# Turns of the identity on TensorE between the spread of g_mix and the first product

## The chip, the cores and the metric

The kernel runs on one core of a Trainium2 chip. The metric is the device time of one execution in microseconds (us). An execution taken with the hardware profiler gives a trace beside its time. "TensorE" multiplies matrices, "VectorE", "ScalarE" and "GpSimd" work on elements, and "SyncE" (SP) issues most of the DMAs; the profile calls them PE (PEld for its weight loads), DVE, ACT, POOL and SP.

## What is computed

One inference step of a trunk of one layer, for a prompt of 2048 frames and a running stream of 32 further frames, 1024 channels each. Cut to what matters here:

```python
hn = rmsnorm(h, g_mix)                 # y = x * rsqrt(mean(x*x) + EPS) * g_mix
proj = hn @ w_in                       # 1024 -> 3072, split into hA, bA, cA, zA, vB, zB
yA, new_conv = short_conv_mixer(hA, bA, cA, zA, conv_hist, conv_w, conv_b)
yB, new_pool = pooling_mixer(vB, zB, pool_hist, pos, pool_w, pool_scale)
h = h + concatenate([yA, yB]) @ w_out
gate = sigmoid(rmsnorm(h, g_ple) @ w_ple_gate)
h = h + (p @ w_ple) * gate             # then a last rmsnorm with g_final
```

The change touches only the beginning: the first `rmsnorm` and the way to the first matmul of `hn @ w_in`.

## The kernel before

**Precision and products.** All inputs are float32. An operand of a product is kept as two float32r numbers, a high half (a cast on ScalarE, line 78) and the rest (a subtraction on VectorE, line 79); the helper `split` makes both and `put` does it for a whole tile. A product then takes three matmuls for each chunk of 128 channels: high with high, high with rest, rest with high. In the input projection the weights stand in the array and 416 frames (`NB`) stream past them.

**Stages.** The 2080 frames are five blocks of 416, in groups of two, two and one (line 26). For each group the program goes through four units (128 channels of each mixer); the first unit of the first group is computed plainly, product by product (`Unit.plain`, line 783): zb and v for the first block, c, then zb, v, c for the second one, then h, za and b for both. Later units use a scheme of seven products for eight. Behind the input projection come the output projection and the gate. TensorE's work is one long row of products from the first one on.

**The beginning.** g_mix is read as one row and spread over the 128 partitions by a matmul with a row of ones, half by half, into `g_bc` (lines 369 to 377):

```python
373   for half in range(2):
374       cs = slice(half * NH, half * NH + NH)
375       pg = tbank(f"gm_{half}")
376       nc.tensor.matmul(pg, ones, gm_row[:, cs], start=True, stop=True)
377       nc.vector.tensor_copy(g_bc[:, cs], pg)
```

The first block is four columns of frames: three of 128 and a short one that holds 32 frames of the first block and 32 of the second (`short0`). Each column is loaded (`x_load`), its sum of squares is taken on ScalarE (line 89) and made into a root on GpSimd (lines 70 and 74), and VectorE scales it by the root and by `g_bc` (`normal`, line 407). TensorE then turns it, since a product needs channels on the partitions: four turns of 128x128 for each half of the channels go into one bank (`turn`, line 416), and `put` splits the bank into the high and low halves in `B0`:

```python
595   for c, x in enumerate([*ahead0, short0]):
596       normal(x)
597       n = P if c < 3 else DEC
598       for half, q in enumerate(("11", "21")):
599           put(B0[q][:, :, :, c * P:c * P + n], turn(x, half, f"pt0_{c}_{half}", bank)[:, :, :n])
```

The first product (`project`, line 581, zb) reads all four columns. It takes its 24 matmuls in the order high-high, frames' rest, weights' rest; all later ones (line 564) go chunk by chunk. The weights of the first three products are split at line 604, behind the columns.

**The second block.** `second_block` (line 610) takes the statistics of three more columns, scales them on VectorE (pinned in order), turns them between the first products of unit 0, splits each bank and also copies it out on ScalarE (line 627).

**PSUM.** There are eight banks: six called "mm" (`bank`, lines 50 and 54) for products and the turns of the two first blocks, and two called "tr" (`tbank`, lines 51 and 57) for the spread of g_mix, the vectors' turn and the pooling products. A bank is handed out again when all its readers are done.

**What sets the order.** Nothing is written out by engine: a scheduler orders the instructions of each engine from the program's order, the dependencies and its own estimate of durations, and places the waits. `tc.keep_in_program_order(ins)` pins an instruction: pinned instructions of an engine keep the order in which the program names them. The function `turn` has the parameter `later`, which pins its turns; the first block's turns don't use it, the second block's do.

Of the kernel before, what the change touches and what calls it, by code (L numbers as in the profile page):

```python
# [15 lines left out]
P = 128  # L16
# [19 lines left out]
def trunk(ctx, tc, x_p, x_s, c_conv, c_pool, p_p, p_s, g_mix, w_in, conv_w, conv_b, pool_w,  # L36
          pool_scale, w_out, g_ple, w_gate, w_ple, g_fin, y_p, y_s, sc_p, sp_p, sc_s, sp_s):
    nc = tc.nc
# [17 lines left out]
    def tbank(name):  # L56
        return ps_t.tile([P, 512], F32, tag="tr", name=name)

    ident = const.tile([P, P], F32, name="ident")
# [17 lines left out]
    def split(hi, lo, src, eng=nc.vector):  # L77
        ins = nc.scalar.copy(hi, src)  # L78
        eng.tensor_tensor(lo, src, hi.bitcast(F32), op=ALU.subtract)
        return ins  # L80
# [24 lines left out]
    def embed(todo, wp, ring, queue=nc.sync):  # L105

        got = {}  # L110

        def prep(c):
            if c in got or c >= len(todo):
                return
            i = todo[c]
            r, n = tiles[i]
            if c % 4 == 0:
                pt = ring("p", i)
                m = min(4, len(todo) - c)
                full = [j for j in todo[c:c + m] if j < NT - 1]  # L120
                if full:
                    nc.sync.dma_start(pt.rearrange("p (a d) -> p a d", a=4)[:, :len(full)],
                                      p_p[r:r + len(full) * P].rearrange("(a p) d -> p a d", p=P))
                if len(full) < m:
                    nc.sync.dma_start(pt[:DEC, len(full) * PLE:(len(full) + 1) * PLE], p_s)
                got["p"] = pt
            pt = got["p"][:, (c % 4) * PLE:(c % 4 + 1) * PLE]
            pps = ring("pps", i)
            ptp = tbank(f"ptp_{i}")
            for k in range(2):  # L130
                nc.tensor.transpose(ptp[:, k * P:k * P + n], pt[:n, k * P:(k + 1) * P], ident[:n, :n])
            v = ptp.rearrange("p (k t) -> p k t", k=4)[:, :2, :n]
            split(pps[:, 0, :, :n], pps[:, 1, :, :n], v)
            got[c] = pps

        def run(c, last=False):
            i = todo[c]
            r, n = tiles[i]
            prep(c)
            prep(c + 1)  # L140
            prep(c + 2)
            pps = got[c]
            o = ring("out", i)
            for nh in range(2):
                cs = slice(nh * NH, nh * NH + NH)
                ps = bank(f"e_{i}_{nh}")
                embed_product(ps, pps, wp, cs, n)
                (nc.vector.tensor_copy if last and nh else nc.scalar.copy)(o[:n, cs], ps[:n])
            (nc.gpsimd if last else queue).dma_start(e_d[r:r + n], o[:n])

        return prep, run
# [141 lines left out]
    def slot(name):  # L293
        return acts[0].tile([P, SLOT], F32R, tag="hn", name=name)
# [30 lines left out]
    def load_rows(pool, name, i, pr, sa=None):  # L325
        r, n = tiles[i]
        t = ring4(pool, f"{name}_{i}")
        nc.sync.dma_start(t[:n], pr[r:r + n] if sa is None else rows_of(pr, sa, r, n))
        return t

    with ExitStack() as s1:
# [10 lines left out]
        def piece_of(t, i):  # L342

            return t[:, i * PIECE:(i + 1) * PIECE].rearrange("p (k h n) -> p k h n", k=KH, h=2)
# [4 lines left out]
        def put(piece, src):  # L349

            return split(piece[:, :, 0], piece[:, :, 1], src)
# [30 lines left out]
        def x_rows(tb, c):  # L382
            r = tb * NB + c * P
            if c < 3:
                return x_p[r:r + P]
            return x_p[r:r + DEC] if tb < 4 else x_s
# [15 lines left out]
        def x_tile(name, rows, squares=junk):  # L402
            return x_stat(x_load(name, rows), squares=squares)

        def normal(x, later=False):
            xt, n, r = x
            ins = nc.vector.scalar_tensor_tensor(xt[:n], xt[:n], r[:n], g_bc[:n], op0=ALU.mult, op1=ALU.mult)
            if later:
                tc.keep_in_program_order(ins)

        def turn(x, half, name, get=tbank, later=False):
            xt, n, _ = x
            pt = get(name)
            for k in range(KH):
                kk = half * KH + k
                ins = nc.tensor.transpose(pt[:, k * P:k * P + n], xt[:n, kk * P:(kk + 1) * P], ident[:n, :n])
                if later:
                    tc.keep_in_program_order(ins)
            return pt.rearrange("p (k t) -> p k t", k=KH)[:, :, :n]
# [70 lines left out]
        def six(g):  # L490

            B = {}
            for i, names in enumerate(SLOTS):
                t = slot(f"B{g}_{i}")
                B.update((q, piece_of(t, c)) for c, q in enumerate(names))
            return B
# [88 lines left out]
        B0 = {}  # L585
# [6 lines left out]
        ahead0 = [x_tile(f"0_{c}", [x_rows(0, c)], in_raw(kind)) for c, kind in enumerate(raw_of)]  # L592
        short0 = x_tile("0_3", [x_rows(0, 3), x_rows(1, 3)])
        B0.update(six(0))
        for c, x in enumerate([*ahead0, short0]):
            normal(x)
            n = P if c < 3 else DEC
            for half, q in enumerate(("11", "21")):
                put(B0[q][:, :, :, c * P:c * P + n], turn(x, half, f"pt0_{c}_{half}", bank)[:, :, :n])
        hn[0] = B0["11"], B0["21"]  # L600
        ahead1 = []
        made = []
# [578 lines left out]
    with ExitStack() as s2:  # L1181
# [112 lines left out]
        for i in range(0, NT - 1, 2):  # L1294
            with tc.issue_after(loaded[-1].ins):
                x = [load_rows(xh, "x", i + b, x_p) for b in range(2)] if i else [first_x, second_x]
# [4 lines left out]
            if last:  # L1301
                n = tiles[NT - 1][1]
# [6 lines left out]
            if last:  # L1309
                x = load_rows(xh, "x", NT - 1, x_p, x_s)  # L1310
# [27 lines left out]
        _, run = embed(rest_e, wp, ring)  # L1338
# [273 lines left out]
        n = tiles[NT - 1][1]  # L1612
# [62 lines left out]
```

## Time and profile before

| what | us |
|---|---|
| three runs | 922.54, 920.85, 921.94 (median 921.94) |
| profiled execution | 920.29 |
| its span, from its first to its last instruction | 918.5 |
| spread of g_mix on TensorE | begins at 2.41 |
| first turn of a column | begins at 8.44 |
| first matmul of the first product | begins at 15.39 |

Times of rows are microseconds from the start of the span. A row of the timeline has its start and length, the engine, the line of the kernel, the operation, what it writes and reads, the shapes, how many such instructions are merged (x8), and in brackets the idle time ahead of it with what ended it. The length of merged rows reaches to the end of the last one, and matmuls overlap. A row of the waits has who waited for whom: the sum in us, the number of times and the longest.

### The profile page before, as it was taken

How to read it: one execution, taken by the hardware profiler on the slowest of the kernel's cores; microseconds unless marked ns; L12 is line 12 of the kernel's file. 1: busy time of each engine (PE TensorE's matmuls, PEld its weight loads, DVE VectorE, ACT ScalarE, POOL GpSimd, SP SyncE). 2: the span in 40 equal slices, each digit the busy share in tenths (PEclk: the TensorE clock that was granted, in tenths of full speed). 3: DMA queues.
4: the chain of work that ended last, by engine and by line, in shares of the span. 5: the costliest groups of instructions: out<-in, count | busy, mean ns of one | idle time of the engine just before them, and what ended most of it. 6: DMA issues, size and time to landing. Idle time of an engine off the chain costs nothing.

```text
span 918.5 us, 12937 instructions
## 1 busy us (share of the span) xinstructions
PE 904.2 (98%) x4485; PEld 819.3 (89%) x4485; DVE 722.4 (79%) x1231; ACT 478.3 (52%) x883; POOL 150.8 (16%) x271
## 2 busy tenths in 40 slices
PE   7999999999999999999999999999999999999996
PEld 5999999999999999999999988888877868888885
DVE  6996989999488989785777679765554799888965
ACT  6744565554345555443545456334334786565555
POOL 4111322212001111000000011111111002233333
PEclk9999999999999999999999999999999999999998
DMA  8245695779935546357655359755785886799893
GB/s 267 80 151 150 163 270 161 201 206 314 415 113 164 184 157 191 110 177 274 200 172 168 130 186 303 260 191 177 247 229 158 290 262 167 187 230 241 210 258 103
DMA packets 140734, 186.37 MB, mean 203 GB/s; under 512 B 12060, under 2 KB 111260, under 8 KB 139389
## 3 DMA queue, kind: packets, MB, share of 16 engines
q1 hardware_dynamic: 120237, 126.33, 45.0%
q0 software_dynamic: 17696, 53.71, 20.1%
q10 hardware_dynamic: 2736, 5.51, 1.8%
q8 instruction: 35, 0.57, 0.3%
q14 instruction: 30, 0.25, 0.1%
HBM read 128.93 MB, written 56.56 MB: 202 GB/s over the span
## 4 chain that ended last, share of the span: by engine, by line
PE 97%; DVE 1%; issue 1%; ACT 0%; DMA 0%; POOL 0%; SPq 0%; ACTq 0%; DVEq 0%; POOLq 0%
PE x_o L168 9%; PE x_g L168 9%; PE x_zbv L564 7%; PE x_ch L564 7%; PE x_zab L564 7%; PE e L103 5%; PE z_g L168 5%; PE z_o L168 4%; PE z_zbv L564 3%; PE z_ch L564 3%; PE z_zab L564 3%; PE v L564 3%; PE c L564 3%; PE b L564 3%; PE za L564 3%; PE h L564 3%
## 5 line engine op out<-in xcount | busy, mean ns | idle before, releaser
L78 ACT CAST y_S<-y_fS 128x512 fp32r<-128x512 f32 x32 | 19.3, 622 | 38.6 <-PE x_o L168 19.0
L103 PE MATMUL e<-wq,pps 128*128 128x512 f32 (+1 forms) x156 | 38.9, 400 | 0.2 <-ACT pps L78 0.2
L168 PE MATMUL x_o<-wo_b,y_S 128*128 128x512 f32 x128 | 35.8, 391 | 0.0
L168 PE MATMUL x_g<-wg_b,g_S 128*128 128x512 f32 x128 | 35.7, 389 | 0.0
L564 PE MATMUL z_zbv<-B,w_zbv_S 128*128 128x416 f32 x168 | 34.2, 352 | 0.0
L564 PE MATMUL x_ch<-B,w_ch_S 128*128 128x416 f32 x168 | 34.1, 351 | 0.0
L564 PE MATMUL z_zab<-B,w_zab_S 128*128 128x416 f32 x168 | 34.1, 351 | 0.0
L564 PE MATMUL x_zab<-B,w_zab_S 128*128 128x416 f32 x168 | 34.0, 351 | 0.0
L564 PE MATMUL x_zbv<-B,w_zbv_S 128*128 128x416 f32 x168 | 34.0, 351 | 0.0
L564 PE MATMUL z_ch<-B,w_ch_S 128*128 128x416 f32 x168 | 34.0, 351 | 0.0
L103 PEld LDWEIGHTS e<-wq,pps 128*128 128x128 f32 (+1 forms) x156 | 27.4, 182 | 7.0 <-ACT pps L78 0.5
L1402 POOL DMA_DIRECT2D e<-h_d x28 | 24.8, 906 | 52.9 <-DVE e L1399 45.9
L564 PEld LDWEIGHTS x_zab<-B,w_zab_S 128*128 128x128 f32 x168 | 31.3, 188 | 0.4
L564 PEld LDWEIGHTS x_zbv<-B,w_zbv_S 128*128 128x128 f32 x168 | 31.4, 188 | 0.3
L564 PEld LDWEIGHTS z_ch<-B,w_ch_S 128*128 128x128 f32 x168 | 31.4, 188 | 0.3
L564 PEld LDWEIGHTS z_zab<-B,w_zab_S 128*128 128x128 f32 x168 | 31.3, 188 | 0.3
L564 PEld LDWEIGHTS x_ch<-B,w_ch_S 128*128 128x128 f32 x168 | 31.3, 188 | 0.3
L564 PEld LDWEIGHTS z_zbv<-B,w_zbv_S 128*128 128x128 f32 x168 | 31.3, 188 | 0.4
L70 POOL TENSOR_SCALAR ms_x<-ssq_x 128x1 f32<-128x1 f32 (+2 forms) x18 | 11.0, 610 | 123.2 <-ACT junk L89 118.7
L78 ACT CAST y<-y 128x512 fp32r<-128x512 f32 x24 | 14.8, 618 | 29.2 <-PE x_o L168 14.6
L78 ACT CAST g_S<-g_fS 128x512 fp32r<-128x512 f32 x32 | 19.0, 618 | 18.5 <-DVE g_fS L1578 11.9
L168 PEld LDWEIGHTS x_o<-wo_b,y_S 128*128 128x128 f32 x128 | 24.0, 188 | 5.1 <-ACT c_o L1205 0.3
(598 smaller groups left out, 2651.5 us busy)
## 6 DMA issues: line engine op xcount, KB each, us to landing
y<-y_d SPq DMA_DIRECT2D x16, 512.0 KB, 5.6
x<-in_x_prompt_dram SPq DMA_DIRECT2D x16, 512.0 KB, 5.6
h_d<-x SPq DMA_DIRECT2D x16, 512.0 KB, 2.6
hn<-h_d SPq DMA_DIRECT2D x61, 128.0 KB, 6.2
xt<-in_x_prompt_dram SPq DMA_DIRECT2D x15, 512.0 KB, 5.4
e<-e_d SPq DMA_DIRECT2D x15, 512.0 KB, 6.4
e<-h_d POOLq DMA_DIRECT2D x28, 256.0 KB, 6.5
out_dram<-e POOLq DMA_DIRECT2D x13, 512.0 KB, 4.2
```

Source lines behind the costliest of these rows:

```text
L70: nc.gpsimd.tensor_scalar(ms[:n], ssq[:n], scalar1=1.0 / D, scalar2=EPS, op0=ALU.mult, op1=ALU.add)
L78: ins = nc.scalar.copy(hi, src)
L103: nc.tensor.matmul(ps[:n], pps[:, a, k, :n], wp[k][b][:, cs], start=k + q == 0, stop=k == 1 and q == 2)
L168: nc.tensor.matmul(ps[:n], lhs[:, k, a, :n], w[b][:, k], start=start and k + q == 0, stop=k == KH - 1 and q == 2, skip_group_check=True)
L564: nc.tensor.matmul(ps[:, :NB], lhs[:, k, x], b[:, k, y], start=start and k + q == 0, stop=stop and k == KH - 1 and q == 2, skip_group_chec ...
L1402: nc.gpsimd.dma_start(ee, h_d[r:r + P, at[1] * NH:at[1] * NH + NH], accum_op=ALU.add)
```

## The change

A bank `idle` is taken from the two "tr" banks, and a function `keep_busy(n)` turns the identity into it n times; nobody reads the result. Ten such turns are placed ahead of the first block's columns, and 5, 8, 10 and 2 behind the turns of the first, second, third and fourth column. They are pinned in the program's order, and so are the turns of the first block's columns from now on.

```diff
         B0.update(six(0))
+        idle = tbank("idle")
+
+        def keep_busy(n):
+
+            for _ in range(n):
+                tc.keep_in_program_order(nc.tensor.transpose(idle[:, :P], ident, ident))
+
+        keep_busy(10)
         for c, x in enumerate([*ahead0, short0]):
             normal(x)
             n = P if c < 3 else DEC
             for half, q in enumerate(("11", "21")):
-                put(B0[q][:, :, :, c * P:c * P + n], turn(x, half, f"pt0_{c}_{half}", bank)[:, :, :n])
+                put(B0[q][:, :, :, c * P:c * P + n], turn(x, half, f"pt0_{c}_{half}", bank, True)[:, :, :n])
+            keep_busy((5, 8, 10, 2)[c])
         hn[0] = B0["11"], B0["21"]
```

## The prediction

> **What bounds the kernel now.** I read the page first, then the waits of TensorE, then its timeline of the first 50 us.
>
> ```profile
> span 918.5 us, 12937 instructions
> PE 904.2 (98%) x4485; PEld 819.3 (89%) x4485; DVE 722.4 (79%) x1231; ACT 478.3 (52%) x883; POOL 150.8 (16%) x271
> ```
> ```profile
> PE gm L376 <- DMA gm_row<-in_g_mix_dram: 2.4, 1, 2.4
> PE pt L416 <- DVE xt L407: 2.3, 1, 2.3
> PE pt L416 <- issue: 1.3, 1, 1.3
> PE x_zab L564 <- DVE U L880: 0.3, 1, 0.3
> PE e L103 <- ACT pps L78: 0.2, 1, 0.2
> ```
> TensorE is busy for 904.2 of 918.5 us. All its waits but the last two, 0.5 us together, lie at the beginning. So whatever makes TensorE's stream earlier after the beginning comes out at the end nearly one for one, and whatever is won ahead of that and met again by another wait is lost.
>
> ```profile
> 2.41 3.75 PE L376 MATMUL gm<-gm_row,ones 1*128 1x512 f32 x4 [2.41 <-DMA gm_row<-in_g_mix_dram]
> 8.44 4.87 PE L416 MATMUL pt<-ident,xt 128*128 128x128 f32 x24 [2.29 <-DVE xt L407]
> 14.61 0.68 PE L416 MATMUL pt<-ident,xt 64*128 64x64 f32 x8 [1.29 <-issue]
> 15.39 2.88 PE L581 MATMUL zb<-B,w_firstzb 128*128 128x416 f32 x8
> 18.07 0.55 PE L564 MATMUL v<-B,w_firstv 128*128 128x416 f32 x1
> 18.41 3.51 PE L581 MATMUL zb<-B,w_firstzb 128*128 128x416 f32 x16
> 21.77 4.50 PE L564 MATMUL v<-B,w_firstv 128*128 128x416 f32 x23
> 26.20 2.60 PE L416 MATMUL pt<-ident,xt 64*128 64x64 f32 x24
> ...
> 28.67 2.52 PE L564 MATMUL c<-B,w_firstc 128*128 128x416 f32 x12
> ...
> 34.17 4.70 PE L564 MATMUL zb<-B,w_firstzb 128*128 128x416 f32 x24
> 38.71 4.70 PE L564 MATMUL v<-B,w_firstv 128*128 128x416 f32 x24
> ```
> The spread of g_mix ends at 2.41 + 3.75 = 6.16 us; the first product, zb, begins at 15.39. Between them stand the turns of four columns of frames, with idle time ahead of them. The second zb product takes 38.71 - 34.17 = 4.54 us for 24 matmuls, 0.189 each. The first one, at 15.39, takes 21.77 - 15.39 = 6.38 us for its 24 and one of v. The windows say why.
>
> ```profile
> 5.48:8.90 3.42, 1.13 (x3) 1.00 1.02 294
> 8.90:12.31 3.41, 3.38 (x17) 1.00 1.16 315
> 12.31:15.72 3.41, 2.01 (x18) 1.00 1.11 346
> 15.72:19.13 3.41, 3.41 (x12) 0.50 0.72 251
> 19.13:22.54 3.41, 3.41 (x20) 1.00 0.77 220
> ```
> The columns are the stretch, its length, TensorE's busy time with its matmuls, the granted clock, the DMA share and GB/s. For 3.41 us, just while the first product runs, the clock is 0.50. The stretch ahead of it, equally long, had TensorE busy for 2.01 of 3.41 us; the stretch ahead of the recovery, for all of it. The column reads 1.00 before that as well, but the weight loads of the turns contradict it:
>
> ```profile
> 10.17 1.57 PEld L416 LDWEIGHTS pt<-ident,xt 128*128 128x128 f32 x8 [0.16 <-DVE xt L407]
> 12.17 0.90 PEld L416 LDWEIGHTS pt<-ident,xt 128*128 128x128 f32 x8 [0.43 <-DVE xt L407]
> 14.57 0.57 PEld L416 LDWEIGHTS pt<-ident,xt 64*128 64x128 f32 x8 [1.50 <-issue]
> ```
> The second column of frames is turned at 1.57 / 8 = 0.20 us a turn, the third at 0.90 / 8 = 0.11, for the same shape. So I read the clock as half from the beginning to about 12.3, full to 15.72 because 8.90 to 12.31 was busy (3.38 of 3.41 us, with turns alone), half again because 12.31 to 15.72 was not, and full from 19.13. The change wants to fill the idle time so that the clock is up before 15.39 and stays up.
>
> The Trainium skill (TensorE: Matmul & The Clock Gate, Part 1) says that the clock is set by a free-running window of about 3.4 us of activity. The stretch of 3.41 us at 0.50 agrees.
>
> **The change part by part.**
>
> *The fill.* Ten turns of the identity follow the spread: at the half-clock price they end at 6.16 + 10 x 0.20 = 8.16, before the first column is ready at 8.44. The stretch 5.48 to 8.90 then holds about 3.1 us of work, and I take the clock to be full from 8.90. The first column: three turns at 0.20 and five at 0.11, to 9.6; five more of the identity to 10.15; the second column from 10.17 to 11.07; eight to 11.95; the third from 12.17 to 13.07; ten to 14.17; the fourth from 14.57 to 15.14; two to 15.36. Each batch ends before the row that follows it in the trace, so the fill costs nothing as long as it runs at 0.11. If the clock rises only at 12.31, each turn of the fill costs 0.20 until then: the second column starts at 10.04 + 1.0 = 11.04 and the first product about 0.9 us late, near 16.3, but warm. What is queued behind a turn of the identity on TensorE is the next column's turns; for those wait ScalarE's casts, VectorE's rests and in the end the product.
>
> Pinning the eight turns of each column into the program's order changes nothing in the sequence that the trace shows. The bank `idle` takes the seat of the first half of the spread; VectorE's copy out of that one must be done, which it is at 5.18:
>
> ```profile
> 4.49 0.69 DVE L377 COPY g_bc<-gm 128x512 f32<-128x512 f32 x1 [2.30 <-PE gm L376]
> ```
> No DMA, no ScalarE and no VectorE instruction is added.
>
> *The first product.* With a full clock, its first eight matmuls run from 15.39 to 15.39 + 8 x 0.189 = 16.90. The next eight read the low halves of the frames, and the last eight the low halves of the weights:
>
> ```profile
> 14.43 2.86 DVE L79 TENSOR_TENSOR B<-pt,B 128x512 fp32r<-128x512 f32 x6
> 17.22 1.27 DVE L79 TENSOR_TENSOR w_firstzb<-raw_firstzb,w_firstzb 128x512 fp32r<-128x512 f32 x2
> ```
> The last low half of the frames is there at 17.29, the one that the first four need a little earlier; I take 17.1. So the second eight end at 18.6, where the weights' rest is already there (18.49), and the third eight at 20.1. The early matmul of v fits into the wait at 16.9. Then v goes on at 20.15 in place of 21.77: 1.6 us are won here. VectorE thus takes back some of what the clock alone would give.
>
> *What is late next.* v's 23 matmuls take 26.20 - 21.77 = 4.43 us, to 24.6; the turns of the second block and the vectors' turn 28.67 - 26.20 = 2.47 us, so c could begin at 27.05. It can't. There are six product banks (line 50): zb, v and six banks of turns have been handed out, so c takes the first bank of turns, and that one must have been read by VectorE and ScalarE. VectorE, however, hangs on another chain:
>
> ```profile
> 25.04 0.55 POOL L74 TENSOR_TENSOR rstd_x<-ms_x,nhalf 128x1 f32<-128x1 f32 x1
> ```
> ```profile
> 25.62 1.28 DVE L407 SCALAR_TENSOR_TENSOR xt<-xt,rstd_x,g_bc 128x1024 f32<-128x1024 f32 x1 [0.72 <-POOL rstd_x L74]
> 26.84 0.59 DVE L752 TENSOR_TENSOR win<-V 128x416 f32<-128x416 f32 x1
> 27.35 0.28 DVE L79 TENSOR_TENSOR B<-pt,B 128x128 fp32r<-128x128 f32 x1
> ...
> 32.95 0.69 DVE L79 TENSOR_TENSOR B<-pt,B 128x512 fp32r<-128x512 f32 x1
> ```
> ```profile
> 28.10 0.28 ACT L627 COPY xt<-pt 128x128 f32<-128x128 f32 x1
> ```
> The last scaling of the second block waits for GpSimd's root at 25.59, which no matmul feeds. It ends at 26.90 whatever TensorE does, and VectorE's work is queued behind it. It reads the bank until 27.63; ScalarE's copy out of the same bank, at 28.10 now, can follow at 27.65 and end at 27.95. So c begins at 28.0 in place of 28.67, and 0.7 of the 1.6 us are left. The second zb product would start at 33.5 in place of 34.17, and its second matmul reads the low half that VectorE finishes at 32.95 + 0.69 = 33.64 now, up to 0.15 earlier when ScalarE's casts come earlier. That leaves 0.5 to 0.7 us; I take 0.6. From there on VectorE's rows have room, and TensorE's only further waits are the 0.5 us above, for results that come from its own products: they move with it.
>
> *Sum.* The profiled execution took 920.29 us, of which the span is 918.5; less 0.6 it is 919.7. The median of the three runs is 921.94, 1.65 above the profiled execution; I take the gain over as it is: 921.3 us. What a measurement of this kernel can tell from no change is about 0.2%, 1.8 us: this gain is below it.
>
> **The unknown price.** No row shows a turn of the identity by itself. The nearest rows are the turns of frames, 0.11 and 0.20 us; I take these. Whether it raises the clock like a turn of frames has two ends. The rows of 8.90 to 12.31 say yes: turns alone, and the loads fall from 0.20 to 0.11. The spread of g_mix, busy from 2.41 to 6.16, says that busy time isn't all: the turns at 8.44 and 10.17 still were slow. It has one row of the array at work, though (1x512), where a turn of the identity has all 128, mostly with zeros. I stay with the nearer row, the turns.
>
> **Rivals.**
>
> *All 1.6 us pass through.* If VectorE's order is drawn up otherwise once TensorE's stream is another (the low halves of the second block ahead of the pooling of v, say), the bank and the second product are freed earlier. Against it stands GpSimd's root at 25.59. Time: 921.94 - 1.6 = 920.3.
>
> *Nothing is won.* The change of clock has its own rhythm of 3.41 us, which need not stand to the program as it does in the profiled execution. Where a stretch ends near 14, it holds most of the second and all of the third column's turns, the clock rises there, and the next stretch, with 15.39 to 17.4 at work, may keep it up: then the old kernel had no cold product. Such runs gain nothing, and if the median run is one, or the bank of c is freed no earlier, the time is 921.9.
>
> *Slower: the fill doesn't count as work for the clock.* Then TensorE stays at 0.20 a turn up to the product and the fill stands in the way. Sum: first column to 10.04, five to 11.04, second column to 12.64, eight to 14.24, third to 15.84, ten to 17.84, the fourth (0.57 us at full clock, 1.1 at half) to 18.94, two to 19.34, and with the fourth column's cast the product at 19.5: 4.1 us later than 15.39, and as cold as it was. All that hangs on the product, VectorE's and ScalarE's work on these columns too, is late by about as much: 926.0. It decides at the point where 8.90 to 12.31, then holding 1.0 us of fill beside the turns of frames, no longer suffices.
>
> The Trainium skill (TensorE: Matmul & The Clock Gate, Part 4) states such a rule: in transpose mode the full clock doesn't engage, since it isn't counted as busy in the same way. By that rule the sum would be this rival's. The trace disagrees as far as turns of frames go: 0.20 us before 12.3, 0.11 after it, with no other work between.
>
> **How the numbers follow.** The forecast, 921.3, has 0.52: every step has a row, the least certain being the bank. Nothing won, 921.9, has 0.22; all of it, 920.3, 0.13; the slower rival, 926.0, 0.13, since one row speaks for turns and none for those of the identity. The likeliest case's own range is that of its bounds, 0.5 to 0.7 us of gain, with the 0.6 us above and the 1.1 below by which the three runs (922.54, 920.85, 921.94) lie about their median: 920.1 to 922.0. The range for all cases reaches from a full gain with some of that scatter, 919.9, to nothing won with the scatter and a delayed fill, 923.2; it leaves out the slower rival and little else. Faster by over 0.2% means below 920.1: half of the full gain's case and a little of the forecast's scatter, 0.12. Slower by over 0.2% means above 923.8: the slower rival and a little, 0.14. Within: 0.74.
>
> **What would show it.** Right: the loads of the third and of the second column at 0.11, no stretch of 0.50 between 12 and 22, the first product's 24 matmuls in about 4.8 us with a wait near 17 for VectorE; c waiting for a bank until about 28.0, and the second zb product at about 33.5. Wrong: turns still at 0.20 at 12 (the slower rival); c at 27.05 and the second zb product at 32.6 (the full gain); the second zb product at 34.2 in spite of a warm first one (another row of VectorE's or ScalarE's holds it); or the order of the instructions on VectorE or ScalarE changed, which would move these rows for a reason that I don't price.

## The result, and the profile after

The changed kernel takes 923.01 us in the median (921.23 to 924.94, 12 runs), the kernel before 921.30 (919.92 to 922.64, 12 runs): a ratio of 1.002, 95% interval 1.0013 to 1.0028. It is slower, by 1.7 us, and the interval is clear of 1; 0.6 us of gain had been forecast. The profiled execution took 924.52 us with a span of 922.8, against 920.29 and 918.5.

The page of the change, its span and its engines:

```profile
span 922.8 us, 13007 instructions
PE 909.2 (99%) x4520; PEld 823.8 (89%) x4520; DVE 723.2 (78%) x1231; ACT 478.2 (52%) x883; POOL 151.3 (16%) x271
```
TensorE has 35 more matmuls and 5.0 us more of busy time (909.2 against 904.2); the other engines have as many instructions as before. Counts cannot show what happened; the waits of TensorE over the whole span of the change do:

```profile
PE pt L416 <- issue: 2.4, 1, 2.4
PE gm L376 <- DVE V L719: 2.3, 1, 2.3
PE x_g L168 <- DVE c_g L1405: 0.4, 1, 0.4
PE x_g L168 <- ACT c_g L1397: 0.3, 1, 0.3
```
Of the three waits of before at this place, the 2.3 us ahead of the first column is filled, as intended. But the one ahead of the short, fourth column, 1.3 us, has become 2.4. (The two of line 168 come late in the program; they are taken up with the second traces below.) TensorE's timeline of the change shows where it stands:

```profile
5.93 2.40 PE L600 MATMUL idle<-ident 128*128 128x128 f32 x10
8.29 1.97 PE L416 MATMUL pt<-ident,xt 128*128 128x128 f32 x8
10.04 1.21 PE L600 MATMUL idle<-ident 128*128 128x128 f32 x5
11.09 1.04 PE L416 MATMUL pt<-ident,xt 128*128 128x128 f32 x8
11.96 1.04 PE L600 MATMUL idle<-ident 128*128 128x128 f32 x8
12.83 1.04 PE L416 MATMUL pt<-ident,xt 128*128 128x128 f32 x8
13.71 1.26 PE L600 MATMUL idle<-ident 128*128 128x128 f32 x10
17.32 0.69 PE L416 MATMUL pt<-ident,xt 64*128 64x64 f32 x8 [2.36 <-issue]
17.94 0.69 PE L600 MATMUL idle<-ident 128*128 128x128 f32 x2
18.28 6.16 PE L581 MATMUL zb<-B,w_firstzb 128*128 128x416 f32 x24
24.28 4.70 PE L564 MATMUL v<-B,w_firstv 128*128 128x416 f32 x24
...
31.54 2.53 PE L564 MATMUL c<-B,w_firstc 128*128 128x416 f32 x12
```
Up to the third column nothing is amiss: its turns end at 13.87, some 0.6 later than before. Then the short column is turned at 17.32 in place of 14.61, the first product begins at 18.28 in place of 15.39, v goes on at 24.28 in place of 21.77 and c at 31.54 in place of 28.67. The product takes 24.28 - 18.28 = 6.0 us again. The windows of the change have the clock:

```profile
11.05:14.46 3.41, 3.41 (x33) 1.00 1.13 332
14.46:17.88 3.42, 1.06 (x13) 1.00 0.95 338
17.88:21.29 3.41, 3.41 (x14) 0.50 0.46 130
```
The fill did bring the clock up ahead of the product: the stretch 11.05 to 14.46 is full of work, and its turns run fast (the eight of the second column take 1.04 us where those of the first took 1.97). In the next one TensorE waits for the short column (1.06 us of work), and the one after it, which holds the product, is at 0.50. So the change has a cold product as before, 2.9 us later.

The label "issue" on the wait names nobody, so the next view is VectorE's timeline, which has the scaling of the columns (L407) and the subtractions that make the rests (L79). First the change:

```profile
11.16 1.29 DVE L407 SCALAR_TENSOR_TENSOR xt<-xt,rstd_x,g_bc 128x1024 f32<-128x1024 f32 x1 [0.93 <-POOL rstd_x L74]
12.37 3.67 DVE L79 TENSOR_TENSOR B<-pt,B 128x512 fp32r<-128x512 f32 x6
15.96 1.27 DVE L407 SCALAR_TENSOR_TENSOR xt<-xt,rstd_x,g_bc 64x1024 f32<-64x1024 f32 x1
```
And the same of before, where the rows from 14.43 on stand in the prediction:

```profile
10.83 1.28 DVE L407 SCALAR_TENSOR_TENSOR xt<-xt,rstd_x,g_bc 128x1024 f32<-128x1024 f32 x1 [0.72 <-POOL rstd_x L74]
12.04 1.28 DVE L79 TENSOR_TENSOR B<-pt,B 128x512 fp32r<-128x512 f32 x2
13.24 1.27 DVE L407 SCALAR_TENSOR_TENSOR xt<-xt,rstd_x,g_bc 64x1024 f32<-64x1024 f32 x1
```
Before, two subtractions stand between the scalings of the third and of the short column, and the other four of the first three columns come behind it. In the change all six stand ahead of it. The short column's scaling begins at 15.96 in place of 13.24, and its turns on TensorE begin 1.4 us later in both (17.32 and 14.61). Its root does not hold it there: GpSimd's row (L74) has it done at 13.71 + 0.54 = 14.25, 1.7 us ahead of the scaling. By itself the later root could explain at most 14.25 - 13.24 = 1.0 of the 2.7 us.

Further on, a wait of TensorE that both kernels have, for the same row, lies near 325 us. In TensorE's timeline of the change that row is:

```profile
327.68 2.53 PE L564 MATMUL x_zab<-B_T,w_zab 128*128 128x416 f32 x12 [0.29 <-DVE U L889]
```
and in that of before:

```profile
324.80 2.54 PE L564 MATMUL x_zab<-B_T,w_zab 128*128 128x416 f32 x12 [0.30 <-DVE U L880]
```
The change is 327.68 - 324.80 = 2.88 us late there, just as at the first product (18.28 - 15.39 = 2.89). This row is the yardstick for the experiments below, since it doesn't feel what happens late in the program.

### The profile page after: what moved, and what is told of

It reads as the page before. It is cut to its first block, busy times and chain, and to the rows that moved or that the text cites. A ratio compares the mean times of both kernels' runs of the same rounds, so it can differ in the third digit from the quotient of the medians.

```text
span 922.8 us, 13007 instructions
## 1 busy us (share of the span) xinstructions
PE 909.2 (99%) x4520; PEld 823.8 (89%) x4520; DVE 723.2 (78%) x1231; ACT 478.2 (52%) x883; POOL 151.3 (16%) x271
## 5 line engine op out<-in xcount | busy, mean ns | idle before, releaser
L168 PEld LDWEIGHTS x_g<-wg_b,g_S 128*128 128x128 f32 x128 | 24.0, 188 | 5.0
```

What stands on the lines that cost most here:

```text
L168: nc.tensor.matmul(ps[:n], lhs[:, k, a, :n], w[b][:, k], start=start and k + q == 0, stop=k == KH - 1 and q == 2, skip_group_check=True)
```

## The experiments

**The theory:** the fill works, and the loss is the order in which the scheduler put VectorE's instructions once TensorE's list had turns of the identity in it. **Its rivals:** the turns of the identity delay TensorE or don't count as work for the clock, so that the fill itself is the loss; or the loss is ScalarE's, whose sum of squares for the short column also comes later (12.21 in place of 10.93 in the traces of the change and of before). A second question is what holds the gain back once the order is right: the bank that c waits for, as the prediction had it.

Each experiment stands against runs of before that were made together with it on the same chip; their medians are 921.24 us for the first four experiments, 921.39 for the next four and 921.55 for the last three. The ratios and intervals are the recorded ones; they differ from the quotient of the two medians by up to 0.0008.

**1. order_kept: the whole fill, with VectorE's order of before.** The statistics of the short column and its scaling are named behind the second column's scaling and ahead of its split, and the casts and subtractions from the second column on are pinned (on ScalarE one cast of the zb weights goes a place earlier than before):

```diff
-        short0 = x_tile("0_3", [x_rows(0, 3), x_rows(1, 3)])
+        short0 = x_load("0_3", [x_rows(0, 3), x_rows(1, 3)])
...
-        for c, x in enumerate([*ahead0, short0]):
-            normal(x)
+        for c in range(4):
+            if c < 3:
+                normal(ahead0[c])
+            if c == 1:
+                short0 = x_stat(short0, True)
+                normal(short0, True)
+            x = [*ahead0, short0][c]
...
+                pins = [nc.scalar.copy(piece[:, :, 0], pt),
+                        nc.vector.tensor_tensor(piece[:, :, 1], pt, piece[:, :, 0].bitcast(F32), op=ALU.subtract)]
+                if c:
+                    for ins in pins:
+                        tc.keep_in_program_order(ins)
```


> The whole fill of the change, but the statistics and the scaling of the short column are named ahead of the second column's split and that split is pinned behind them, so that VectorE's instructions stand in the order of the kernel before. Theory A (the change lost its time because VectorE's scaling of the short column was put behind six subtractions in place of two; the fill itself does no harm and raises the clock): the first product begins near 15.4 us, no stretch at half clock on it, the second zb product at 33.4 to 33.7; time 0.3 to 1.0 us below the kernel before. Theory B (the fill stands in the way of the turns, whatever the order): the first product begins at 16.3 or later and the time is 1 to 2 us above the kernel before.

Measured: 920.74 us (919.67 to 922.00, 11 runs), ratio 0.9997, interval 0.9987 to 1.0006; profiled 920.32, span 918.5. VectorE has the order of before again:

```profile
12.38 1.28 DVE L614 TENSOR_TENSOR B<-pt,B 128x512 fp32r<-128x512 f32 x2
13.58 1.27 DVE L407 SCALAR_TENSOR_TENSOR xt<-xt,rstd_x,g_bc 64x1024 f32<-64x1024 f32 x1
```
TensorE's timeline of order_kept:

```profile
13.45 1.25 PE L600 MATMUL idle<-ident 128*128 128x128 f32 x10
14.94 0.68 PE L416 MATMUL pt<-ident,xt 64*128 64x64 f32 x8 [0.24 <-issue]
15.75 5.05 PE L581 MATMUL zb<-B,w_firstzb 128*128 128x416 f32 x24
20.63 4.69 PE L564 MATMUL v<-B,w_firstv 128*128 128x416 f32 x24
...
28.30 2.55 PE L564 MATMUL c<-B,w_firstc 128*128 128x416 f32 x12 [0.35 <-ACT xt L646]
...
33.83 4.70 PE L564 MATMUL zb<-B,w_firstzb 128*128 128x416 f32 x24
...
324.44 2.53 PE L564 MATMUL x_zab<-B_T,w_zab 128*128 128x416 f32 x12 [0.29 <-DVE U L899]
```
The same 35 turns of the identity, and the loss is gone: the yardstick stands at 324.44, 0.36 us earlier than before's. The clock rises at 9.32, where the loads of a turn shorten from 0.20 to 0.11 us, and the granted clock doesn't fall until the end of TensorE's work; the product takes 20.63 - 15.75 = 4.88 us. Of the 1.14 us that v is earlier, c leaves 0.37 (28.30 in place of 28.67), and it waits for ScalarE's copy out of a bank of turns (L646, the line that is L627 in before). That is the prediction's chain, and the fill is cleared of the loss. A gain over before is not shown by the times: the interval includes 1.

**2. short_late: the order alone, without a fill.** One word in the kernel before: the short column's scaling is pinned. A pinned instruction comes behind the one that the program names just before it on its engine, here the sixth subtraction.

```diff
         for c, x in enumerate([*ahead0, short0]):
-            normal(x)
+            normal(x, c == 3)
```


> The kernel before, without any fill; one pin puts the scaling of the short column behind the six subtractions of the first three columns. Theory A: the order alone costs what the change cost: the short column's turns near 17, the first product near 18, TensorE idle for about 3.5 us ahead of it and the product at half clock for a part; 1.5 to 3 us above the kernel before. Theory B: within 0.5 us of the kernel before.

Measured: 924.60 us (923.90 to 926.02, 5 runs), ratio 1.0044, interval 1.0031 to 1.0056; that is 3.4 us above before, somewhat more than the 1.5 to 3 expected. VectorE's timeline of short_late has the order of the change:

```profile
12.43 3.67 DVE L79 TENSOR_TENSOR B<-pt,B 128x512 fp32r<-128x512 f32 x6
16.02 1.26 DVE L407 SCALAR_TENSOR_TENSOR xt<-xt,rstd_x,g_bc 64x1024 f32<-64x1024 f32 x1
```
and TensorE's is:

```profile
8.48 6.06 PE L416 MATMUL pt<-ident,xt 128*128 128x128 f32 x24 [2.28 <-DVE xt L407]
17.39 0.79 PE L416 MATMUL pt<-ident,xt 64*128 64x64 f32 x8 [2.85 <-issue]
18.17 6.19 PE L581 MATMUL zb<-B,w_firstzb 128*128 128x416 f32 x24
...
327.43 2.53 PE L564 MATMUL x_zab<-B_T,w_zab 128*128 128x416 f32 x12 [0.29 <-DVE U L880]
```
Without one turn of the identity the rows of the change come back: the short column at 17.39, a product from 18.17 to 24.20 and the yardstick 2.63 us late. ScalarE takes the sum of squares early here (11.13) and the root is there at 13.18, so the second rival falls too: VectorE's six subtractions are enough. (The clock rises only at 14.40 in this trace, so all three columns are turned at the half-clock price; VectorE's six subtractions stand without a gap from 12.43 all the same.)

**3. fill_32: the change with 32 turns behind the third column in place of 10,** to keep TensorE at work while the short column is late:

```diff
-            keep_busy((5, 8, 10, 2)[c])
+            keep_busy((5, 8, 32, 2)[c])
```


> The change with 32 turns of the identity in place of 10 behind the third column, so that the wait for the short column is filled too. It keeps the change's order on VectorE. If turns of the identity count as work for the clock: a stretch of about 3.4 us with nothing but these turns is followed by the full clock, the first product takes 4.6 to 5 us in place of 6.0, beginning near 18.3, and the time lies 0.3 to 1.5 us below the change. If they don't: half clock on the first product as in the change, and the change's time or up to 0.7 us more.

Measured: 923.88 us (921.41 to 926.65, 9 runs), ratio 1.0029, interval 1.0015 to 1.0044; profiled 921.60, span 919.8. Its TensorE timeline:

```profile
13.30 3.66 PE L600 MATMUL idle<-ident 128*128 128x128 f32 x32
17.17 0.68 PE L416 MATMUL pt<-ident,xt 64*128 64x64 f32 x8 [0.22 <-issue]
...
17.98 4.78 PE L581 MATMUL zb<-B,w_firstzb 128*128 128x416 f32 x24
22.59 4.69 PE L564 MATMUL v<-B,w_firstv 128*128 128x416 f32 x24
...
325.80 2.53 PE L564 MATMUL x_zab<-B_T,w_zab 128*128 128x416 f32 x12 [0.30 <-DVE U L889]
```
and the windows of fill_32:

```profile
10.14:13.55 3.41, 3.41 (x33) 1.00 1.09 326
13.55:16.97 3.42, 3.40 (x32) 1.00 1.11 361
16.97:20.38 3.41, 3.21 (x23) 1.00 0.53 163
```
The stretch 13.55 to 16.97 holds turns of the identity and nothing else, and the next one stays at 1.00. This settles the prediction's unknown price: for the clock, these turns of the identity are work. The product begins as late as in the change but takes 4.61 us in place of 6.00, and the yardstick is 1.0 us behind before's in place of 2.9. So in the change's rows, the order costs about 2.9 us and a warm product would give about 1.9 of it back. The times disagree with the rows here: the median was expected 0.3 to 1.5 us below the change's and lies 0.9 above it. The profiled execution is one of the fastest of the nine, and none of the others was traced (see 11).

**4. one_turn: a single turn of the identity ahead of the columns, none behind them.**

```diff
-        keep_busy(10)
+        keep_busy(1)
...
-            keep_busy((5, 8, 10, 2)[c])
+            keep_busy((0, 0, 0, 0)[c])
```


> The change with a single turn of the identity ahead of the first column and none elsewhere: nothing that fills idle time is left, but the order on VectorE is that of the change. Theory A: the short column's turns near 17, the first product near 18, and 1.5 to 3 us above the kernel before. Theory B: within 0.5 us of the kernel before, since 0.2 us of fill lies in idle time.

Measured: 923.77 us (923.61 to 924.28, 4 runs), ratio 1.0034, interval 1.0021 to 1.0048. VectorE's timeline of one_turn:

```profile
12.26 3.67 DVE L79 TENSOR_TENSOR B<-pt,B 128x512 fp32r<-128x512 f32 x6
15.85 1.26 DVE L407 SCALAR_TENSOR_TENSOR xt<-xt,rstd_x,g_bc 64x1024 f32<-64x1024 f32 x1
```
One turn on TensorE, 0.47 us in a stretch in which it waits otherwise, is enough to turn VectorE's order. TensorE's product begins at 18.00 and the yardstick stands at 327.93, 3.1 us late.

**5. c_own_bank: order_kept, and the first product c takes a "tr" bank** in place of the first bank of turns:

```diff
-                def product_of(kind, b, w, between=None):
-                    ps = bank(f"{kind}{tag}_{tbs[b]}")
+                def product_of(kind, b, w, between=None, get=bank):
+                    ps = get(f"{kind}{tag}_{tbs[b]}")
...
-                    nc.scalar.copy(self.cols(c_s, b), product_of("c", b, wc, between))
+                    nc.scalar.copy(self.cols(c_s, b), product_of("c", b, wc, between, bank if b else tbank))
```


> The kernel of order_kept with the first product of c in one of the two other PSUM banks, so that it needn't wait for the first turned bank of the second block to be read. If that bank is what gave back most of the gain: c begins right behind the vectors' turn (27.7 to 28.0 in place of 28.30), with no wait on ScalarE's copy ahead of it, and the second zb product at 33.2 to 33.7, now held by VectorE's low halves (33.69); 0.1 to 0.6 us below order_kept, less than the runs can tell apart. If the bank was not it: the second zb product at 33.8 as in order_kept.

Measured: 920.25 us (919.47 to 922.77, 11 runs), ratio 0.9991, interval 0.9982 to 0.9999; profiled 920.04. TensorE's timeline of c_own_bank:

```profile
27.57 2.52 PE L564 MATMUL c<-B,w_firstc 128*128 128x416 f32 x12
...
33.07 0.35 PE L564 MATMUL zb<-B,w_firstzb 128*128 128x416 f32 x1
33.62 4.61 PE L564 MATMUL zb<-B,w_firstzb 128*128 128x416 f32 x23 [0.19 <-DVE B L79]
```
The bank was the hold: c begins at 27.57 without a wait. The next hold is the one that the prediction named, VectorE's low half: the second zb product stops after its first matmul and goes on at 33.62. The yardstick stands at 324.14, 0.66 us earlier than before's.

**6. pw_early: c_own_bank, and the split of the pooling weights moved ahead,** between VectorE's scalings of the second block, so that VectorE has less to do behind GpSimd's last root:

```diff
-            for x, _ in xs:
+            for i, (x, _) in enumerate(xs):
                 normal(x, True)
+                if i == 0:
+                    nc.scalar.copy(pw[:, 0], pw_raw)
+                    tc.keep_in_program_order(nc.vector.tensor_tensor(pw[:, 1], pw_raw, pw[:, 0].bitcast(F32), op=ALU.subtract))
...
+        pw = one.tile([P, 2, 4, P], F32R, name="pw")
+        pw_raw = raws.tile([P, 4, P], F32, tag="t", name="raw_pw")
+        nc.sync.dma_start(pw_raw, pool_w[0].rearrange("g c d -> c g d"))
         second = second_block()
...
-            split(pw[:, 0], pw[:, 1], pw_raw)
```


> c_own_bank, and besides the split of the pooling weights is moved into the time in which VectorE waits for GpSimd's roots (between the scalings of the second block), so that 0.6 us less work stands ahead of the second block's low halves. If VectorE's row of work is what holds the second zb product: it begins at 32.9 to 33.3, and the time is 0.7 to 1.2 us below the kernel before. If something else holds it: 33.5 or later.

Measured: 920.20 us (919.34 to 922.99, 12 runs), ratio 0.9987, interval 0.9978 to 0.9996. In its trace the columns began later and the product stands at 16.46, 0.6 us behind that of c_own_bank; the second zb product begins at 33.70 and runs without a stop, and the yardstick is 324.30. It is the fastest of all versions by its median, but its interval overlaps that of c_own_bank. Whether the moved split adds anything stays open: the 32.9 to 33.3 expected for the second zb product was not reached, but this trace started its first product late.

**7 and 8. before_again and change_again: one more trace of each kernel,** to see what the rows of one execution are worth.

> The kernel before once more, for the phase of the clock. If the half-clock stretch comes from a rhythm that isn't tied to the program, it begins at another instant than 15.72 us of the span, by up to 3.4 us, or is missing; if it is tied to the program, at 15.7 again. The first turn of a column at about 8.4, the first product at about 15.4.

> The change once more. The order of the instructions is fixed, so the short column's turns stand near 17.3 and the first product near 18.3 again; the half-clock stretch begins at another instant than 18.25, as far as its rhythm is not tied to the program. Waits of the gate stage (1.0 us in the first profile) may or may not come back; if they don't, they are not the change's.

Measured: before 923.00 us, change 925.89. The yardstick repeats: 324.88 and 327.90, 3.0 us apart. The clock's stretches don't stand still: in before the product's half clock runs from 15.03 to 18.44 in place of 15.72 to 19.13, in the change from 18.73 to 22.14 in place of 17.88 to 21.29 (the 18.25 of the expectation is not where the first trace has it). All four last 3.41 us and all four lie on the first product. This run of before is 2.7 us longer than the first one. At the yardstick it is only 0.08 us late, and the rest arises between 760 and 870 us; about half of it is one wait of TensorE, where the first trace has none from 745 us on:

```profile
PE x_g L168 <- DVE c_g L1396: 1.3, 1, 1.3
```
The other half comes in smaller steps of the same stage. It is the gate stage, far from the change. Such waits differ from run to run of the same kernel: pw_early's trace has one of 1.8 us, at 922.99 us against a median of 920.20; the change's has two, 0.7 us together. The two profiled executions differ by 4.23 us, of which 2.88 are there at the yardstick; the other 1.35 arise in this stage, which is a reason to trust a profiled execution's time less than its early rows.

**9. no_first_ten: the change without the ten turns ahead of the first column,** those behind the columns kept (`keep_busy(10)` becomes `keep_busy(0)`).

> The change without the ten turns ahead of the first column; the 5, 8, 10 and 2 behind the columns stay. In its compiled order the short column's scaling stands behind two subtractions, as before the change. Theory A: the product begins at 15.4 to 15.9, and TensorE stands 0 to 0.7 us ahead of the kernel before at the wait near 324 us. Theory B (fill harms by itself): the product later than 16 and TensorE 0.5 us or more behind at 324.

Measured: 921.85 us (921.17 to 923.06, 10 runs), ratio 1.0006, interval 0.9996 to 1.0015. VectorE's timeline of no_first_ten has the order of before at this place:

```profile
12.29 1.28 DVE L79 TENSOR_TENSOR B<-pt,B 128x512 fp32r<-128x512 f32 x2
13.49 1.26 DVE L407 SCALAR_TENSOR_TENSOR xt<-xt,rstd_x,g_bc 64x1024 f32<-64x1024 f32 x1
```
TensorE's product runs warm, from 16.47 to 21.12, c waits 0.37 us for its bank and begins at 28.82, and the yardstick is 324.95. So it is the turns ahead of the first column that change VectorE's order, one of them or ten; the pins on the columns' turns, which no_first_ten has too, do not. The gain expected at the yardstick (0 to 0.7 us) did not come. The product begins 0.6 us later than the latest time expected: the five turns of the identity behind the first column run before the clock rises (their loads take 1.08 us together), and ScalarE has two casts of v's weights (15.09) ahead of the short column's casts (16.13). And further on VectorE has the rest of the pooling weights (27.07) ahead of the subtraction that reads c's bank, which stands at 28.18 in place of 27.35.

**10 and 11. order_kept_again and fill_32_again: one more trace of each.**

> order_kept once more, for the scatter of its parts: the product at 15.4 to 15.9 at full clock, c waiting for its bank until 28.0 to 28.4, the second zb product at 33.5 to 33.9, and the wait near 324 us at 323.5 to 324.0.

> fill_32 once more, since its runs spread from 921.4 to 926.7. If the clock or the fill makes the spread: another start of the product than 17.98, or half clock on it. If the spread comes from the gate stage: the product near 18 at full clock again, the wait near 324 us at 325.2 again, and the waits between 745 and 880 us larger than in the first look, which had none.

Measured: 920.24 and 921.42 us; the yardstick 324.37 and 326.00 (324.44 and 325.80 in the first traces), no half clock in either before the end. In order_kept_again c (28.22) and the second zb product (33.74) stand where they were expected, but the first product begins at 16.22, later than expected, and the yardstick misses its 323.5 to 324.0. With a warm product in both kernels the order thus costs 1.4 to 1.6 us at the yardstick (fill_32 against order_kept), not 2.9. Both traces of fill_32 come from the fast end of its runs and have no late wait, so where its slower runs, up to 926.65, lose their time stays open.

The versions by their yardstick row and their time:

| kernel | VectorE's order | fill | yardstick, us | median, us | ratio (interval) |
|---|---|---|---|---|---|
| before | two, then short | none | 324.80 / 324.88 | 921.30 | |
| change | six, then short | 10; 5, 8, 10, 2 | 327.68 / 327.90 | 923.01 | 1.0020 (1.0013 to 1.0028) |
| short_late | six, then short | none | 327.43 | 924.60 | 1.0044 (1.0031 to 1.0056) |
| one_turn | six, then short | 1; 0, 0, 0, 0 | 327.93 | 923.77 | 1.0034 (1.0021 to 1.0048) |
| fill_32 | six, then short | 10; 5, 8, 32, 2 | 325.80 / 326.00 | 923.88 | 1.0029 (1.0015 to 1.0044) |
| no_first_ten | two, then short | 0; 5, 8, 10, 2 | 324.95 | 921.85 | 1.0006 (0.9996 to 1.0015) |
| order_kept | two, then short | 10; 5, 8, 10, 2 | 324.44 / 324.37 | 920.74 | 0.9997 (0.9987 to 1.0006) |
| c_own_bank | two, then short | 10; 5, 8, 10, 2 | 324.14 | 920.25 | 0.9991 (0.9982 to 0.9999) |
| pw_early | two, then short | 10; 5, 8, 10, 2 | 324.30 | 920.20 | 0.9987 (0.9978 to 0.9996) |

Every kernel with the order of six has an interval above 1, none with the order of two has.

## Why the prediction was wrong

**The step that failed** is the one about what the pins and turns do to the rest: "changes nothing in the sequence that the trace shows", and "No DMA, no ScalarE and no VectorE instruction is added". The first was said of the pins, and no_first_ten, which has them too, keeps VectorE's order at this place. The second is true (1231 and 883 instructions in both), and it was taken to mean that those engines' order stays. It doesn't: the scheduler places the instructions of all engines, and one added turn put four more subtractions, 3.67 us for six against 1.28 for two, ahead of the scaling that the product waits for. short_late, with that order alone, lost 2.6 us at the yardstick; order_kept, with the fill alone, won 0.36. The short column's turns came at 17.32 where the prediction has them at 14.57, and the forecast gain of 0.6 us became a loss of 1.7. The prediction's list of signs named a changed order, "for a reason that I don't price", and gave it no chance: the mistake is that it was not made a rival. That 923.01 us lies inside the outer range, 919.9 to 923.2, is luck: none of the cases from which that range was drawn has this order.

**The clock.** Read rightly: half from the beginning, up after a stretch full of turns, down after one that was not full (2.01 of 3.41 us in before, 1.06 of 3.42 in the change). "I take the clock to be full from 8.90", with 12.31 as the other case: of the traces with turns behind the columns, it rose at 9.32 in one and between 10.1 and 12.1 in the others; the later end was the likelier one. So "the fill costs nothing as long as it runs at 0.11" came with too early a rise: before it each turn costs 0.20 us, and the first product came at 16.22 in order_kept_again, near the 16.3, "but warm", of the other case. The product was warm in both traces of order_kept and in that of no_first_ten.

**The slower rival, "the fill doesn't count as work for the clock",** was on the right side for a wrong reason: fill_32 refutes its mechanism for these turns. The rule of the Trainium skill (TensorE: Matmul & The Clock Gate, Part 4), that in transpose mode the full clock doesn't engage, is not borne out by them: the rows have turns alone ahead of a rise and ahead of a full stretch. The profile lists these turns as MATMUL and doesn't show whether the mode that the page means was set.

**"Nothing is won", for a clock whose rhythm isn't tied to the program:** the rhythm is indeed free (15.72 in one trace of before, 15.03 in the other), but both traces of before had the cold product. Its other runs have only their mean granted clock on record, and that speaks for this rival's premise. The six traces with a cold product (before, the change, short_late, one_turn) have means of 0.995 to 0.997, the seven with a warm one 0.997 to 0.999; half of 3.41 us out of 920 makes 0.0019. Of the 55 runs of before that were made with the experiments, 24 have 0.998 or 0.999; of the nine of short_late and one_turn none has. So many runs of before probably had a warm product without any fill. No trace shows one.

**The chain behind the product,** seen in order_kept, came out nearly as worked out: the product's warm length 4.88 us (forecast 20.15 - 15.39 = 4.76); c held by ScalarE's copy out of the first bank of turns until 28.30 (forecast 28.0); the second zb product at 33.83 (33.5), and behind it VectorE's low half (c_own_bank). The gain is 0.36 to 0.51 us at the yardstick, over two traces of each kernel, where 0.6 was taken. In the first trace of order_kept VectorE's last scaling of the second block, from which the bank is counted, stood at 25.96 in place of 25.62; before_again has 25.92, so this is scatter between executions and not a cost of the fill. "All 1.6 us pass through" fell with the bank and the low half, as its own counter-argument had it: c_own_bank, without the bank's hold, wins 0.66.

**What stays open.** Why the scheduler's choice flips on a turn ahead of the first column and not on the turns behind the columns: nothing here shows how it weighs them. Also open is why the medians lie 1.7 us apart where TensorE's rows lie 2.9. A likely part of the answer is that the change, too, was not cold in every run. From the yardstick to the end of the span the thirteen traces take 593.7 to 596.9 us. The change's fastest run has a span of 919.5 us, so its yardstick stood at 919.5 - 593.7 = 325.8 or earlier, unless its end was shorter than any traced one; both traces of the change have it near 327.8. A warm product is worth about these 1.9 us in the change (fill_32), but only about 0.4 in before, where the bank of c holds it back (order_kept). Three of the change's twelve runs have a mean granted clock of 0.998 or 0.999, above every trace with a cold product. This is an estimate from the recorded spans and clocks; no trace shows a run of the change with a warm product.

## What to carry to other kernels

Where a scheduler orders the engines, an instruction added to one of them can move the work of another, even if nobody reads its result: compare every engine's order before and after, or pin what the critical path hangs on, before pricing the added work. Filling idle time to keep the clock up helps only as far as the next hold, so follow each gain to the buffer or engine that is late next (here a bank, then VectorE). And compare kernels at one row that both have, close behind the edit, rather than by the end of one execution.

## What the runs showed of the hardware

The clock is read here in stretches of 3.41 us, counted back and forth from a change of the granted clock. Its column reads 1.00 ahead of the first change, so there the length of the loads is the evidence.

Turns of the identity, whose operands are nearly all zeros, keep the clock up: 32 of them alone filled the stretch 13.55 to 16.97 of fill_32, and the next stretch was at 1.00. The length of work is not all, though. The spread of g_mix, with one row of the array, kept TensorE busy for the whole of the stretch 2.50 to 5.91 of order_kept, as the profile counts it, and yet the ten turns behind it had loads of 0.20 us each; the clock rose only at 9.32, after a stretch of turns. In the change, the spread and turns filled 4.22 to 7.63, and the clock rose only at 11.05.

How full a stretch has to be is known between two bounds only. Busy for 3.13 of 3.41 us with turns, it was followed by the full clock (before_again, 8.21 to 11.62); busy for 2.46 it was not (short_late, 7.57 to 10.98).

Each of the six half-clock stretches on the first product measured 3.41 or 3.42 us, and where it begins differs by up to 0.9 us between two traces of one kernel.
